# Merge with tokens on partitions, the three products of a weight chunk sorted, and the retention output's transposes placed later

## The chip, the cores and the metric

The kernel runs on one core of one Trainium2 chip. The metric is the device time of one execution in microseconds (us); smaller is better. Before the change three executions took 2119.16, 2122.03 and 2122.19 us, median 2122.03.

The engines are named as in the profile: PE is TensorE's matrix multiply and PEld its weight load, DVE is VectorE, ACT is ScalarE, SP issues the transfers. A matrix product on PE has a stationary operand (128 x 128, put into the array by a weight load) and a moving operand (128 x N, streamed through it); the result stands in PSUM with the stationary operand's columns on its partitions.

## What is computed

Two layers over 256 tokens of width 2048. In each layer one normalised input `h` feeds two branches, retention (8 heads) and latent attention (16 heads); each branch has its own projection back to 2048 columns, the two are gated by sigmoids, summed, and projected once more:

```
proj = h @ w_in
rq, rk, rv, rg, cq, ckv, kr, mg, bg = jnp.split(proj, points, axis=-1)
o_ret = head_group_norm(retention(rq, rk, rv)).reshape(B, S, RET_V_W)
y_ret = (o_ret * jax.nn.silu(rg)) @ w_ret_proj
...
y_mla = (o_mla * jax.nn.silu(mg)) @ w_mla_proj
g_a, g_b = jnp.split(jax.nn.sigmoid(bg), 2, axis=-1)
merged = g_a * y_ret + g_b * y_mla
out = merged @ w_out
return x + gate[:, None, :] * out
```

All is f32.

## The kernel before

**Products in three parts.** Every weight and every activation is split into a rounded part (`hi`, of type fp32r) and the rest (`lo`). `mm3` (L258) makes a product out of three: hi·hi (L260), hi·lo (L261) and lo·hi (L262), all added in the same place of PSUM.

**Weights come in chunks.** `load_split` (L246) fetches one chunk of 512 KB into a tile `wst` (a pool of 5, L237), ACT writes its hi half (L241) and DVE its lo half (L242) into a tile `whl` (a pool of 3). A chunk is two row blocks of 128 by 512 columns. SP issues all transfers of weights in program order.

**Two layouts.** `proj` (L274) takes a 128 x 128 block of weights as the stationary operand and streams the 256 tokens: results have features on partitions, and a chunk makes 24 products of 256 columns (2 row blocks x 4 column blocks x 3). `proj_tok` (L282) takes 128 tokens of the activation as the stationary operand and streams 512 columns of weights: results have tokens on partitions, and a chunk makes 12 products of 512 columns (2 row blocks x 2 token halves x 3). Before the change `proj_tok` makes the retention values and gates (`rv`, `rg`) and most of the last output; `proj` makes the rest: the gate columns `C_BA` (tiles `ma`, L480), the retention projection (`branch_a`, L639), the gate columns `C_BB` (L873) and the attention projection (L877). Each of these four takes 4 pieces of 512 columns, each of 8 chunks, in either layer.

**Order of the work.** The code is written in program order and a scheduler then orders each engine's instructions by a simulated time. In a layer come: the first products (`first_products`, L580; it makes 14 of 16 column groups, two of them `ma`), then the retention of four pairs of heads (`g` = 0 to 3, L703 to L752), with other products between (`run(PLAN[...])`: `a` is `gate_a`, `b` is `branch_a`, `q`, `r` and `v` belong to attention), then the attention heads, then the merge (L870 to L882), then `w_out`. After its head pair's norm and gate (`rv*rg`, L743), retention turns its result by eight transposes on PE (L749), whose outcome is split into the tiles `z` (L750). `PLAN[4]` is `"a3 b0 b1 b2 b3"`; `branch_a` needs the `z` of all four pairs, the last one for its chunks 7 and 8.

**Background.** In layer 0 `bg()` puts pieces of the modulation's product (`w_mod`, `mod_slice` L400: one load into `wst`, two DVE instructions at L341 into `macc`) between the chunks, 0.6 of one to each chunk while the `b` projections run and 0.5 in the merge.

Of the kernel before, what the change touches and what calls it, by code (L numbers as in the profile page):

```python
# [17 lines left out]
P = 128  # L18
# [90 lines left out]
def trunk(ctx: ExitStack, tc: tile.TileContext, x, c, positions, w_mod, b_mod, g_norm, w_in, g_cq,  # L109
# [153 lines left out]

    def proj_chunk(accs, hi, lo, k0, nk, span, act):

        for k in range(nk):
            kt = k0 + k
            for j in range(hi.shape[2] // P):
                cs = slice(j * P, (j + 1) * P)
                mm3(accs[j // 2][:, j % 2, :], (hi[:, k, cs], lo[:, k, cs]),  # L270
                    act.block(kt),
                    start=(kt == span[0] and j % 2 == 0), stop=(kt == span[1] - 1))
# [9 lines left out]
    def proj_tok(w, col, act, span=(0, KT)):  # L282

        accs = [acc_tile() for _ in range(2)]
        for k0 in range(*span, 2):
            hi, lo = load_split(w[k0 * P : (k0 + 2) * P, col : col + 512], 2, 512)
            for k in range(2):
                kt = k0 + k
                for t in range(2):
                    mm3(accs[t].rearrange("p a b -> p (a b)"), act.block(kt, slice(t * P, (t + 1) * P)),  # L290
                        (hi[:, k, :], lo[:, k, :]), start=kt == span[0], stop=kt == span[1] - 1)
        return [a.rearrange("p a b -> p (a b)") for a in accs]
# [175 lines left out]
    class Slots(dict):  # L468


        def __missing__(self, key):
            self[key] = (tokens if key[0] in ("rv", "rg") else blocks)(key[0])
            return self[key]

    def ret_proj(W, n, hh, span=(0, KT)):
# [3 lines left out]
        if n >= 12:  # L479
            return proj(W, C_BA + (n - 12) * 512, 512, hh, span)  # L480
        return proj_tok(W, C_RV + (n - 4) * 512, hh, span)

    def ret_dst(tiles, n):
# [4 lines left out]
        if n >= 12:  # L488
            return [tiles["ma", n - 12][:, 2 * a : 2 * a + 2, :] for a in range(2)]
        t = tiles[("rv", n - 4) if n < 8 else ("rg", n - 8)]  # L490
# [120 lines left out]
    def layer(l, r, u):  # L611
# [90 lines left out]

        for sg in range(2):  # L703
            for which in range(2):
                get(2 * sg + which, rope_pair)
            run(PLAN[2 * sg])
            for pr in range(2):
# [36 lines left out]
                for h in range(2):  # L744
                    ps = aux_tile()
                    for e in range(2):
                        for t in range(2):
                            f = h * S + e * P
                            T.transpose(ps[:, e * S + t * P : e * S + (t + 1) * P], rv[:, t, f : f + P], ident)  # L749
                    split_into(*zz.flat(2 * g + h), ps)  # L750
                if pr == 0:
                    run(PLAN[2 * sg + 1])  # L752

# [7 lines left out]
        for name in PLAN[4:]:  # L761
            run(name)
# [6 lines left out]
        for g in range(MH // 2):  # L769
# [12 lines left out]
            for k0 in (0, 2):  # L782
# [6 lines left out]
                split_into(hr, lr, w[:, :, :, NOPE:])  # L789
                for k in range(2):  # L790
                    kt = k0 + k
                    b = cq.block(kt)
                    for h in range(2):
                        mm3(a1[:, h, :], (hn[:, k, h, :], ln[:, k, h, :]), b, kt == 0 and h == 0, kt == 3)
                    mm3(a2[:, 0, :], tuple(u[:, k].rearrange("p h d -> p (h d)") for u in (hr, lr)), b, kt == 0, kt == 3)
# [5 lines left out]
            for k0 in (0, 2):  # L801
                hi, lo = load_split(w_ukv[l, k0 * P : (k0 + 2) * P, g * 512 : (g + 1) * 512], 2, 512)
                for k in range(2):
# [3 lines left out]
                    for h in range(2):  # L807
                        mm3(a1[:, h, :], (hv[:, h, :NOPE], lv[:, h, :NOPE]), b, kt == 0 and h == 0, kt == 3)
                    for t in range(2):
                        ts = slice(t * P, (t + 1) * P)  # L810
# [193 lines left out]
```

## Time and profile before

| | |
|---|---|
| median of three runs | 2122.03 us |
| the profiled execution's own time | 2121.04 us |
| its span in the profile | 2119.2 us |
| PE busy | 2067.8 us, 98% of the span |
| DVE, ACT busy | 1505.7 us (71%), 1062.0 us (50%) |
| transfers | 460.99 MB, mean 218 GB/s |

A product's row gives its own duration from first column to last result. Products overlap, so the pace is read from the start of one to the start of the next, or from the number of products in a stretch in which PE never rests.

### The profile page before, as it was taken

The numbers are of one execution on the slowest core, as the hardware profiler recorded it, in microseconds if no ns is written. First come the engines' busy times: TensorE is split into PE (matmuls) and PEld (weight loads), VectorE is DVE, ScalarE is ACT, GpSimd is POOL, SyncE is SP. The second block draws the span as 40 slices with busy tenths as digits, with TensorE's granted clock in tenths as the row PEclk, the third lists the DMA queues.
The fourth block names the chain that finished last, engine by engine and source line by source line (L and its number), as shares of the span: only waits on it lengthen the run. The fifth ranks groups of instructions, "written<-read, shape, count | busy, mean of one in ns | idle before, by whom it ended". The sixth has DMA issues, their size and how long they took to land.

```text
span 2119.2 us, 37911 instructions
## 1 busy us (share of the span) xinstructions
PE 2067.8 (98%) x15418; PEld 1964.6 (93%) x15422; DVE 1505.7 (71%) x2258; ACT 1062.0 (50%) x1485; POOL 0.2 (0%) x4
## 2 busy tenths in 40 slices
PE   7999999998999999999999999999999999999998
PEld 4898898998999999999998799899999999999987
DVE  5789987677677876775577776657766777754464
ACT  4554356543356664444454464445443666644453
POOL 0000000000000000000000000000000000000000
PEclk9999999999999999999999999999999999999999
DMA  8988866566766667776569976665567666666572
GB/s 309 313 297 284 296 188 186 160 200 209 265 207 195 184 204 239 254 257 194 184 182 326 311 218 186 189 180 157 185 221 225 186 193 195 204 216 186 181 240 97
DMA packets 263535, 460.99 MB, mean 218 GB/s; under 512 B 18464, under 2 KB 68032, under 8 KB 263360
## 3 DMA queue, kind: packets, MB, share of 16 engines
q1 hardware_dynamic: 263360, 458.57, 68.8%
q8 instruction: 121, 1.98, 0.4%
q14 instruction: 54, 0.44, 0.1%
HBM read 456.41 MB, written 2.10 MB: 216 GB/s over the span
## 4 chain that ended last, share of the span: by engine, by line
PE 72%; DMA 14%; DVE 9%; issue 3%; ACT 1%; SPq 0%; ACTq 0%; DVEq 0%
PE acc L261 22%; PE acc L262 22%; PE acc L260 22%; DMA wst<-in_w_mod 9%; DMA ring<-in_w_mod 4%; DVE whl L242 4%; DVE macc L341 2%; DMA wmod<-in_w_mod 1%; DVE tmp L341 1%; ACT whl L241 1%; PE aux L262 1%; PE aux L261 1%; PE aux L260 1%; DVE extra L341 0%; PE aux L857 0%
## 5 line engine op out<-in xcount | busy, mean ns | idle before, releaser
L241 ACT ACTIVATE whl<-wst 128x1024 fp32r<-128x1024 f32 (+1 forms) x708 | 707.9, 1006 | 821.2 <-PE acc L262 674.1
L242 DVE TENSOR_TENSOR whl<-wst,whl 128x1024 fp32r<-128x1024 f32 (+1 forms) x708 | 812.6, 1155 | 310.8 <-ACT whl L241 309.3
L260 PE MATMUL acc<-h,whl 128*128 128x256 f32 x2272 | 645.2, 285 | 3.8 <-DVE qkn L465 1.2
L261 PE MATMUL acc<-h,whl 128*128 128x256 f32 x2272 | 643.6, 284 | 0.8 <-DVE h L242 0.8
L262 PE MATMUL acc<-h,whl 128*128 128x256 f32 x2272 | 638.6, 284 | 2.4 <-DVE whl L242 2.2
L260 PEld LDWEIGHTS acc<-h,whl 128*128 128x128 f32 x2272 | 436.2, 192 | 6.0 <-ACT h L241 1.6
L261 PEld LDWEIGHTS acc<-h,whl 128*128 128x128 f32 x2272 | 436.5, 192 | 2.0 <-DVE h L242 1.4
L262 PEld LDWEIGHTS acc<-h,whl 128*128 128x128 f32 x2272 | 433.5, 192 | 3.9 <-DVE whl L242 3.8
L262 PE MATMUL acc<-z,whl 128*128 128x256 f32 x1024 | 291.5, 285 | 6.5 <-DVE whl L242 6.4
L261 PE MATMUL acc<-z,whl 128*128 128x256 f32 x1024 | 291.1, 285 | 2.6 <-DVE z L242 2.6
L260 PE MATMUL acc<-z,whl 128*128 128x256 f32 x1024 | 291.4, 285 | 1.7 <-ACT ma L622 1.7
L341 DVE SCALAR_TENSOR_TENSOR macc<-wst,cact,macc 128x512 f32<-128x512 f32 x180 | 134.9, 749 | 133.4 <-DMA wst<-in_w_mod 131.3
L261 PE MATMUL acc<-whl,h 128*128 128x512 f32 x512 | 203.6, 398 | 3.2 <-DVE whl L242 3.1
L262 PEld LDWEIGHTS acc<-z,whl 128*128 128x128 f32 x1024 | 197.1, 193 | 8.6 <-DVE whl L242 8.4
L261 PEld LDWEIGHTS acc<-z,whl 128*128 128x128 f32 x1024 | 197.5, 193 | 2.9 <-DVE z L242 2.8
L262 PE MATMUL acc<-whl,h 128*128 128x512 f32 x512 | 200.1, 391 | 0.0
L260 PEld LDWEIGHTS acc<-z,whl 128*128 128x128 f32 x1024 | 197.3, 193 | 2.1 <-ACT ma L622 2.0
L260 PE MATMUL acc<-whl,h 128*128 128x512 f32 x512 | 181.0, 391 | 0.0
L341 DVE SCALAR_TENSOR_TENSOR tmp<-ring,cact,tmp 128x512 f32<-128x512 f32 x150 | 112.2, 750 | 44.7 <-DMA ring<-in_w_mod 43.1
L261 PEld LDWEIGHTS acc<-whl,h 128*128 128x128 f32 x512 | 96.2, 188 | 26.5 <-DVE whl L242 7.2
L260 PEld LDWEIGHTS acc<-whl,h 128*128 128x128 f32 x512 | 96.0, 188 | 19.8
L262 PEld LDWEIGHTS acc<-whl,h 128*128 128x128 f32 x512 | 96.3, 188 | 19.2
(265 smaller groups left out, 2701.2 us busy)
## 6 DMA issues: line engine op xcount, KB each, us to landing
wst<-in_w_in SPq DMA_DIRECT2D x416, 512.0 KB, 4.4
wst<-in_w_mod SPq DMA_DIRECT2D x96, 512.0 KB, 4.2
ring<-in_w_mod SPq DMA_DIRECT2D x80, 512.0 KB, 5.2
wst<-in_w_ret_proj SPq DMA_DIRECT2D x64, 512.0 KB, 5.0
wst<-in_w_mla_proj SPq DMA_DIRECT2D x64, 512.0 KB, 4.9
wst<-in_w_out SPq DMA_DIRECT2D x64, 512.0 KB, 4.8
wst<-in_w_ukv SPq DMA_DIRECT2D x32, 512.0 KB, 3.9
wst<-in_w_uq SPq DMA_DIRECT2D x32, 384.0 KB, 4.2
```

What stands on the lines that cost most here:

```text
L241: A.activation(hi, src, AF.Copy)
L242: V.tensor_tensor(lo, src, hi.bitcast(F32), ALU.subtract)
L260: T.matmul(o, a[0], b[0], start=start, stop=False, skip_group_check=True)
L261: T.matmul(o, a[0], b[1], start=False, stop=False, skip_group_check=True)
L262: T.matmul(o, a[1], b[0], start=False, stop=stop, skip_group_check=True)
L341: V.scalar_tensor_tensor(acc, w[:, k, :], cact[:, k0 + k : k0 + k + 1], acc, ALU.mult, ALU.add)
```

## The change

It has four parts. (1) `ma`, the retention projection, the `C_BB` gates and the attention projection use `proj_tok`. (2) The merge then has its sum with tokens on partitions, and turns it by eight transposes for each piece of 512 columns before it is split into `m`; before, no transposes were needed. (3) `chunk` replaces `mm3` for weights: for a whole chunk first all products with the hi half of the weights (L270), then all with the lo half (L273). (4) Retention's transposes move into `turn`, called later in the program: for pairs 0 and 2 after `run(PLAN[2 * sg + 1])`, for pair 1 after the `q` product, for pair 3 after `a3`.

```diff
+    def chunk(todo):
+        for o, w, a, start, _, moves in todo:
+            for i in range(2):
+                x, y = (a[i], w[0]) if moves else (w[0], a[i])
+                T.matmul(o, x, y, start=start and i == 0, stop=False, skip_group_check=True)
+        for o, w, a, _, stop, moves in todo:
+            x, y = (a[0], w[1]) if moves else (w[1], a[0])
+            T.matmul(o, x, y, start=False, stop=stop, skip_group_check=True)
...
-        if n >= 12:
-            return proj(W, C_BA + (n - 12) * 512, 512, hh, span)
-        return proj_tok(W, C_RV + (n - 4) * 512, hh, span)
+        return proj_tok(W, C_RV + (n - 4) * 512 if n < 12 else C_BA + (n - 12) * 512, hh, span)
...
-            accs = proj(w_ret_proj[l], n * 512, 512, zz)
-            for a in range(2):
-                s2 = ma[:, 2 * a : 2 * a + 2, :]
-                V.tensor_tensor(s2, s2, accs[a], ALU.mult)
+            for t, acc in enumerate(proj_tok(w_ret_proj[l], n * 512, zz)):
+                V.tensor_tensor(ma[:, t, :], ma[:, t, :], acc, ALU.mult)
...
+        def turn(g):
+            for h in range(2):
+                ps = aux_tile()
+                for e in range(2):
+                    for t in range(2):
+                        f = h * S + e * P
+                        T.transpose(ps[:, e * S + t * P : e * S + (t + 1) * P], tiles["rv", g][:, t, f : f + P], ident)
+                split_into(*zz.flat(2 * g + h), ps)
...
             run(PLAN[2 * sg])
+            if sg:
+                turn(1)
...
                 V.tensor_tensor(rv, rv, rg, ALU.mult)
-                for h in range(2):
-                    ps = aux_tile()
...
                 if pr == 0:
                     run(PLAN[2 * sg + 1])
+                    turn(g)
...
-        for name in PLAN[4:]:
-            run(name)
+        last, *rest = PLAN[4].split()
+        run(last)
+        turn(3)
+        run(" ".join(rest))
...
-            accs = proj(W, C_BB + n * 512, 512, hh)
             gb = [tmp_tile(), tmp_tile()]
+            for t, acc in enumerate(proj_tok(W, C_BB + n * 512, hh)):
+                A.activation(gb[t], acc, AF.Sigmoid)
+            for t, acc in enumerate(proj_tok(w_mla_proj[l], n * 512, zz)):
+                V.tensor_tensor(gb[t], gb[t], acc, ALU.mult)
+                V.tensor_tensor(gb[t], gb[t], tiles["ma", n][:, t, :], ALU.add)
             for a in range(2):
-                A.activation(gb[a], accs[a].rearrange("p a b -> p (a b)"), AF.Sigmoid)
-            accs = proj(w_mla_proj[l], n * 512, 512, zz)
...
+                ps = aux_tile()
+                for b in range(2):
+                    f = (2 * a + b) * P
+                    for t in range(2):
+                        T.transpose(ps[:, b * S + t * P : b * S + (t + 1) * P], gb[t][:, f : f + P], ident)
+                split_into(*mm.flat(2 * n + a), ps)
```

The other users of `mm3` on weights (`proj_chunk`, `proj_tok`, the two products of an attention head pair, the last output's third piece) call `chunk` in the same way.

How the instructions stand is shown at three places. First PE in layer 0, around the transposes of the last head pair (g = 3). Before, the last products of `b0`'s sixth chunk stand ahead of them:

```order
L260 MATMUL acc<-z,whl 128x256
L261 MATMUL acc<-z,whl 128x256
L262 MATMUL acc<-z,whl 128x256
L749 MATMUL aux<-cst,rv 128x128 x8
L347 LDWEIGHTS part
```

After (L270 is hi, L273 is lo, L737 is the last score product of this pair, L709 the transposes):

```order
L737 MATMUL aux<-rv,tmp 128x256
L270 MATMUL acc<-whl,z 128x512 x4
L273 MATMUL acc<-whl,z 128x512 x4
L270 MATMUL acc<-whl,z 128x512 x8
L273 MATMUL acc<-whl,z 128x512 x4
L270 MATMUL acc<-whl,z 128x512 x8
L273 MATMUL acc<-whl,z 128x512 x4
L270 MATMUL acc<-whl,z 128x512 x8
L273 MATMUL acc<-whl,z 128x512 x4
L709 MATMUL aux<-cst,rv 128x128 x8
```

Before, 83 products of 256 columns stood between the last score product (L726) and the transposes; now 44 of 512 columns do, and as 84 `z` products now stand ahead of the transposes, where `b0` has 72 that need no `z` of the last pair, one chunk of `b1` has come ahead of them.

Second, DVE at the same place. Before, the gate product `rv*rg` (L743), for which the transposes wait, stands behind a background row (L341):

```order
L741 TENSOR_SCALAR rv<-rv,small 128x256 x4
L242 TENSOR_TENSOR whl<-wst,whl 128x1024
L341 SCALAR_TENSOR_TENSOR macc<-wst,cact,macc 128x512
L743 TENSOR_TENSOR rv<-rv,rg 128x1024
L242 TENSOR_TENSOR whl<-wst,whl 128x1024
```

After (L346 is the background row, L752 and L754 the norm and `rv*rg`):

```order
L346 SCALAR_TENSOR_TENSOR macc<-wst,cact,macc 128x512
L752 TENSOR_SCALAR rv<-rv,small 128x256 x4
L242 TENSOR_TENSOR whl<-wst,whl 128x1024
L754 TENSOR_TENSOR rv<-rv,rg 128x1024
L346 SCALAR_TENSOR_TENSOR macc<-wst,cact,macc 128x512 x2
L242 TENSOR_TENSOR whl<-wst,whl 128x1024
```

The background row now stands ahead of the norm, and two more stand between `rv*rg` and the next weight split.

Third, PE where the merge of layer 0 goes from its first piece to the second. Before, the products of the attention projection (`z`) were followed at once by those of the next gates (`h`), and no transposes stood there. After (L895 are the new transposes, L352 background sums):

```order
L273 MATMUL acc<-whl,z 128x512 x4
L270 MATMUL acc<-whl,h 128x512 x8
L273 MATMUL acc<-whl,h 128x512 x4
L270 MATMUL acc<-whl,h 128x512 x8
L273 MATMUL acc<-whl,h 128x512 x4
L270 MATMUL acc<-whl,h 128x512 x6
L895 MATMUL aux<-cst,tmp 128x128 x2
L270 MATMUL acc<-whl,h 128x512 x2
L352 LDWEIGHTS part
L352 MATMUL aux<-ones_h,part 128x1
L273 MATMUL acc<-whl,h 128x512 x4
```

Two transposes stand behind 30 products of the next gates' first three chunks, the other six a little later. In the whole program 6144 products of 256 columns are gone and 3072 of 512 columns and 64 transposes are new.

## Rows read from the trace of the kernel before

**Rows 1.** Page, part 1: busy us, share of the span, instructions.

```profile
PE 2067.8 (98%) x15418; PEld 1964.6 (93%) x15422; DVE 1505.7 (71%) x2258; ACT 1062.0 (50%) x1485; POOL 0.2 (0%) x4
```

**Rows 2.** Groups of PE products by shape: busy us, mean ns | idle before.

```profile
L260 PE MATMUL acc<-h,whl 128*128 128x256 f32 x2272 | 645.2, 285 | 3.8 <-DVE qkn L465 1.2 <-ACT h L241 0.9 <-ACT h L543 0.9
...
L261 PE MATMUL acc<-whl,h 128*128 128x512 f32 x512 | 203.6, 398 | 3.2 <-DVE whl L242 3.1
```

**Rows 3.** Stretches holding one width of product only, then one with late weights.

```profile
core 0: us, PE busy (x) PEld busy (x) DVE busy (x) ACT busy (x) POOL busy (x), PEclk, DMA share, GB/s
1890.00:2010.00 120.00, 120.00 (x1002) 120.00 (x1001) 58.08 (x54) 49.62 (x52) 0.00 (x0) 1.00 0.62 184
150.00:180.00 30.00, 30.00 (x134) 24.87 (x133) 28.04 (x36) 11.70 (x11) 0.00 (x0) 1.00 0.93 312
...
1180.00:1224.00 44.00, 42.08 (x183) 33.69 (x182) 33.29 (x41) 19.27 (x22) 0.00 (x0) 1.00 0.92 315
```

**Rows 4.** PE in order of time around eight transposes in layer 1.

```profile
1541.12 0.28 PE L262 MATMUL acc<-z,whl 128*128 128x256 f32 x1
1541.24 1.04 PE L749 MATMUL aux<-cst,rv 128*128 128x128 f32 x8
1542.03 0.36 PE L260 MATMUL acc<-z,whl 128*128 128x256 f32 x1
1542.23 0.29 PE L261 MATMUL acc<-z,whl 128*128 128x256 f32 x1
```

**Rows 5.** Waits: us in total, times, longest us.

```profile
ACT whl L241 <- PE acc L262: 674.1, 387, 5.5
...
DVE macc L341 <- DMA wst<-in_w_mod: 131.3, 70, 4.5
...
PEld acc L262 <- DVE whl L242: 12.2, 17, 2.1
...
PE acc L262 <- DVE whl L242: 8.7, 12, 1.9
...
PEld acc L261 <- DVE whl L242: 7.2, 11, 1.7
...
ACT whl L241 <- DMA wst<-in_w_mla_proj: 4.2, 2, 2.6
...
PE acc L261 <- DVE whl L242: 3.1, 4, 1.3
...
ACT whl L241 <- DMA wst<-in_w_ret_proj: 2.8, 1, 2.8
```

**Rows 6.** PE's groups in layer 0 from 498 to 516 us.

```profile
L260 PE MATMUL acc<-z,whl 128*128 128x256 f32 x21 | 7.0, 342 | 1.7 <-ACT ma L622 1.7
L261 PE MATMUL acc<-z,whl 128*128 128x256 f32 x21 | 6.7, 321 | 0.0
L262 PE MATMUL acc<-z,whl 128*128 128x256 f32 x21 | 6.6, 317 | 0.0
L749 PE MATMUL aux<-cst,rv 128*128 128x128 f32 x8 | 2.0, 428 | 4.5 <-DVE rv L743 4.5
L347 PE MATMUL aux<-ones_h,part 128*128 128x1 bf16 x12 | 0.5, 169 | 0.0
```

**Rows 7.** DVE in order of time at that place.

```profile
502.59 1.22 DVE L242 TENSOR_TENSOR whl<-wst,whl 128x1024 fp32r<-128x1024 f32 x1
504.85 0.75 DVE L341 SCALAR_TENSOR_TENSOR macc<-wst,cact,macc 128x512 f32<-128x512 f32 x1 [1.04 <-DMA wst<-in_w_mod]
505.52 1.22 DVE L743 TENSOR_TENSOR rv<-rv,rg 128x1024 f32<-128x1024 f32 x1
```

**Rows 8.** Stretches of layer 0: that place, two of the `b` projections, one of the merge.

```profile
498.00:516.00 18.00, 11.80 (x83) 11.24 (x82) 12.94 (x23) 6.47 (x8) 0.00 (x0) 0.72 0.68 215
516.00:550.00 34.00, 34.00 (x294) 33.96 (x294) 25.29 (x31) 13.88 (x14) 0.00 (x0) 1.00 0.71 231
550.00:590.00 40.00, 37.12 (x316) 36.67 (x315) 25.48 (x31) 14.57 (x17) 0.00 (x0) 1.00 0.79 259
860.00:900.00 40.00, 37.91 (x312) 37.35 (x311) 24.95 (x29) 14.79 (x16) 0.00 (x0) 1.00 0.80 264
1134.00:1168.00 34.00, 34.00 (x152) 28.16 (x151) 27.37 (x32) 16.33 (x20) 0.00 (x0) 1.00 0.96 331
```

**Rows 9.** Groups of DVE and ACT in the merge and in the splits.

```profile
L242 DVE TENSOR_TENSOR whl<-wst,whl 128x1024 fp32r<-128x1024 f32 x636 | 774.4, 1222 | 307.8 <-ACT whl L241 306.3
...
L879 DVE TENSOR_TENSOR tmp<-tmp,acc 128x512 f32<-128x512 f32 x16 | 10.7, 684 | 0.0
...
L880 DVE TENSOR_TENSOR tmp<-tmp,ma 128x512 f32<-128x512 f32 x16 | 10.6, 686 | 0.0
```

More of the change, by code (lines that the diff above doesn't have):

```diff
@@ L262, in mm3 @@
         T.matmul(o, a[1], b[0], start=False, stop=stop, skip_group_check=True)
-    def proj_chunk(accs, hi, lo, k0, nk, span, act):
[L266 to L272, printed above, removed]
+    def chunk(todo):
[6 more added lines that the diff above has]
+            T.matmul(o, x, y, start=False, stop=stop, skip_group_check=True)
+    def proj_chunk(accs, hi, lo, k0, nk, span, act):
+        chunk([(accs[j // 2][:, j % 2, :], (hi[:, k, j * P : (j + 1) * P], lo[:, k, j * P : (j + 1) * P]),
+                act.block(k0 + k), k0 + k == span[0] and j % 2 == 0, k0 + k == span[1] - 1, False)
+               for k in range(nk) for j in range(hi.shape[2] // P)])
     def proj(w, col, n, act, span=(0, KT)):
@@ L286, in proj_tok @@
             hi, lo = load_split(w[k0 * P : (k0 + 2) * P, col : col + 512], 2, 512)
[L287 to L291, printed above, removed]
+            chunk([(accs[t].rearrange("p a b -> p (a b)"), (hi[:, k, :], lo[:, k, :]),
+                    act.block(k0 + k, slice(t * P, (t + 1) * P)), k0 + k == span[0], k0 + k == span[1] - 1, True)
+                   for k in range(2) for t in range(2)])
         return [a.rearrange("p a b -> p (a b)") for a in accs]
@@ L487, in ret_dst @@
             return [tiles["qk", n // 2 * 2 + a][:, f : f + 2, :] for a in range(2)]
-        if n >= 12:
-            return [tiles["ma", n - 12][:, 2 * a : 2 * a + 2, :] for a in range(2)]
-        t = tiles[("rv", n - 4) if n < 8 else ("rg", n - 8)]
+        t = tiles[("rv", n - 4) if n < 8 else ("rg", n - 8) if n < 12 else ("ma", n - 12)]
         return [t[:, a, :] for a in range(2)]
@@ L793, in layer @@
                     for h in range(2):
-                        mm3(a1[:, h, :], (hn[:, k, h, :], ln[:, k, h, :]), b, kt == 0 and h == 0, kt == 3)
-                    mm3(a2[:, 0, :], tuple(u[:, k].rearrange("p h d -> p (h d)") for u in (hr, lr)), b, kt == 0, kt == 3)
+                        todo.append((a1[:, h, :], (hn[:, k, h, :], ln[:, k, h, :]), b, kt == 0 and h == 0, kt == 3, False))
+                    w = [u[:, k].rearrange("p h d -> p (h d)") for u in (hr, lr)]
+                    todo.append((a2[:, 0, :], w, b, kt == 0, kt == 3, False))
+                chunk(todo)
             A.activation(qn, a1[:, :, 0:P], AF.Copy)
@@ L807, in layer @@
                     for h in range(2):
[L808 removed]
+                        todo.append((a1[:, h, :], (hv[:, h, :NOPE], lv[:, h, :NOPE]), b, kt == 0 and h == 0, kt == 3, False))
                     for t in range(2):
[L810 to L812 removed]
+                        todo.append((a2[:, t, :], (hv[:, :, NOPE:], lv[:, :, NOPE:]),
+                                     [u[:, t * P : (t + 1) * P] for u in b], kt == 0 and t == 0, kt == 3, True))
+                chunk(todo)
             A.activation(kn, a1[:, :, 0:P], AF.Copy)
@@ L949, in last_output @@
             hi, lo = load_split(w[k0 * P : (k0 + 4) * P, c0 : c0 + 256], 4, 256)
-            for k in range(k0, k0 + 4):
-                for t in range(2):
-                    mm3(accs[t], mm.block(k, slice(t * P, (t + 1) * P)), (hi[:, k - k0], lo[:, k - k0]), k == 0, k == KT - 1)
+            chunk([(accs[t], (hi[:, k - k0], lo[:, k - k0]), mm.block(k, slice(t * P, (t + 1) * P)), k == 0, k == KT - 1, True)
+                   for k in range(k0, k0 + 4) for t in range(2)])
         for t in range(2):
```

16 lines of the change are left out of this document (3 added, 13 removed).

## The prediction

> **What bounds the kernel now.** I read the engines' busy shares first, then PE's groups, then stretches with a single kind of product, then the waits, then the one place where PE rests long.
>
> PE is busy for 98% of the span, DVE for 71%, ACT for 50% [rows 1]. A busy PE says little by itself, because a product's row (285 ns for 256 columns, 398 ns for 512) is longer than its share of the stream [rows 2]. So I take the pace from stretches that hold one kind only and in which PE never rests [rows 3]. In the first, 1002 products of 256 columns touch 120 us; the row also counts those that only reach over the edges, about two, so the pace is 120/1000 = 0.120 us. In the second, 134 products of 512 columns touch 30 us, which gives 30/132.3 = 0.2268 us. The two stretches have the same clock (1.00) and very different transfer rates (184 and 312 GB/s), so neither is waiting for weights. At 0.120 us a chunk of 24 narrow products takes 2.88 us, against 1.06 us of ACT and 1.22 us of DVE for its split [rows 9].
>
> The waits say the same: ACT waits 674.1 us in total for PE to give a weight tile back, so weights normally lie ready [rows 5]. The kernel is bound by PE's stream of products; other things matter only where they make it pause. The pauses are few: those for DVE's half of the weights (`whl`) add up to 11.8 us as PE's idle time (8.7 and 3.1) or 19.4 us as its weight loads see them (12.2 and 7.2), and one place in layer 0, at 498 to 516 us, stands out [rows 5, 6, 8].
>
> **Wide products for narrow ones.** 6144 products of 256 columns become 3072 of 512 with the same arithmetic. Two narrow ones take 0.2400 us, a wide one 0.2268 us: 0.0132 us saved 3072 times is **40.6 us**. The new products have just the form of those in the second stretch (activation stationary, `whl` streamed), so I take its pace. The ends are 0.226 us (about 43 us saved) and the pace of the third stretch of [rows 3], where wide products wait for weights: 44/181.3 = 0.243 us, at which nothing is saved. The stretches in question are nearer to the first end: in the `b` projections and the merge PE's idle time is 0 to 2.9 us in 34 to 40 us [rows 8].
>
> The Trainium skill, "TensorE: Matmul & The Clock Gate", section "Back-to-back issue gap", gives for a product alone columns/2.4 + 2.5 ns when the clock is full, which is 109.2 and 215.8 ns. By it a pair would save only 2.5 ns, 7.7 us in all. The trace differs: both widths run 11 ns above it, and it is this constant, paid once where it was paid twice, that makes most of the 40.6 us.
>
> **The merge's transposes.** Eight for each of four pieces in two layers: 64 on PE. Between the product that starts at 1541.12 and the one at 1542.23 lie 1.11 us; they hold eight transposes and two products' shares, so the eight take 1.11 - 0.24 = 0.87 us, 0.109 us each [rows 4]. That is **7.0 us** more of PE's stream. Below nothing is excluded, since it is added work on the full engine.
>
> The same page, section "Part 4: PE-mode transpose", tells of some 275 ns for one in a kernel. That speaks against the change and would make 17.6 us of the 7.0. Here 1.04 us for a row of eight contradicts it as a pace.
>
> The transposes also add a wait: PE stands still until DVE has summed, and behind them on PE stand the next piece's products, for which ACT and DVE wait in turn. In layer 0, 30 products (6.8 us) stand between the last product and the first two transposes, and 36 (8.2 us) before the other six. DVE's chain for all of it is two multiplications, a sum, a weight split, a background subtraction (taken as 0.69 us like the sum), a sum: 2 x 0.684 + 0.686 + 1.222 + 0.69 + 0.686 = 4.65 us, the first sum after 2.05 us [rows 9]. So 3.5 us of slack are left. The work on DVE and ACT does not change otherwise: the same number of multiplications, sums and splits of the same size.
>
> **The sorted chunk.** Before, DVE's half is needed at the second or third product, 0.23 or 0.24 us after the chunk begins. Now it is needed after 16 narrow (1.92 us) or 8 wide ones (1.81 us), some 1.6 us later. The waits for it are 2.1 us at the longest and mostly below 1 us (12.2 us in 17) [rows 5], so nearly all go. The bounds are 0, if ACT's half is late at the same places, and 19.4 us; I take **14 us**, between the two readings. Number and order of loads on SP stay nearly the same, so no transfer starts later by it.
>
> **Retention's transposes.** They wait for DVE only at one place: pair 3 of layer 0, 4.5 us [rows 6]. DVE's `rv*rg` stood there behind a background row that waited 1.04 us for its transfer [rows 7], and the granted clock fell: 0.72 on the mean of these 18 us [rows 8]. At full pace the work in it would take 63 x 0.120 + 0.87 + 0.5 = 8.9 us, so the place costs 9.1 us [rows 6]. The name of the change promises cover here, but the order of instructions gives little: 83 narrow products stood between the last score product and the transposes (10.0 us), now 44 wide ones do (10.0 us). What does change is DVE's order, in which the background row comes before the norm; against that, one chunk of `b1` now stands ahead of the transposes, whose split is queued behind two more background rows. The bounds are 0 and 9.1 us; I take **4 us** saved.
>
> Elsewhere the transposes already start behind finished work, and moving them gains nothing. For pair 3 of layer 1 the cover shrinks, from 115 narrow products (13.8 us) to 48 wide ones (10.9 us). With this and the eight new waits in the merge I put **3 us** of new pauses into the sum, bounds 0 and 12 (1.5 us each, the size of a mean wait for a background transfer, 131.3/70 = 1.9 us, less what slack takes).
>
> **The sum.** 2121.0 - 40.6 + 7.0 - 14 - 4 + 3 = 2072.4 us for the profiled execution. The median of the runs lies 1.0 above it, so 2073.
>
> **Rivals.**
>
> *Pauses only move (chance 0.20).* Sorting and later transposes gain nothing net; the counts of products remain: 2121.0 - 40.6 + 7.0 + 3 = 2090. For it: DVE's lateness comes from transfers (131.3 us of waiting [rows 5]), which the change leaves alone.
>
> *Weights set the pace (0.12): no gain.* A wide chunk takes 12 x 0.2268 = 2.72 us instead of 2.88, so the same transfers must come 6% faster. If `wst` tiles come free too late, chunks keep their old pace, the saving is nil and the transposes fall into the waits: about 2115 to 2121. For it: ACT does wait for some loads (2.8 and 4.2 us [rows 5]) and PE rests in two of the stretches. Against: 259 GB/s would become 275, and the trace has 331 GB/s with PE busy throughout [rows 8].
>
> *The merge's transposes stop PE (0.07): slower.* If DVE is over 3.5 us late at each of the eight, because background rows ahead of the sums wait for transfers (4.5 us at the longest [rows 5]), and each such stop brings the clock down as at 498 us, each costs 9.1 us: 2072.4 - 3 + 8 x 9.1 = 2142. The change is slower from 6.4 us each (51.6/8) on. Against: mean waits of 1.9 us stay below the slack.
>
> *The forecast (0.61)*, own range 2060 to 2086.
>
> **How the numbers follow.** The low end takes all bounds of a gain, 2121.0 - 43 + 7.0 - 19.4 - 9.1 = 2056. The high end leaves half the saving and no gain of pauses: 2121.0 - 20 + 7.0 = 2108. That leaves out most of the second and all of the third rival, and so under 2 in 10. A measurement of this kernel tells about 0.2% (4 us) from no change. Faster: the forecast, the first rival and most of the second, 0.90; same: the rest of the second, 0.04; slower: 0.06.
>
> **What the profile of the changed kernel would show.** The wide groups' pace in undisturbed stretches of the `b` projections near 0.227 us, else the first term is wrong. PE's waits for DVE's `whl` down from 11.8 us to 1 or 2, else sorting missed its mark. At pair 3 of layer 0, a wait for `rv*rg` below 4.5 us and a granted clock that stays at 1.00; a mean as low as 0.72 there would say that nothing was gained. The new transposes' idle time below 3 us in all. ACT waiting for `wst` transfers for tens of us would speak for the second rival. The prediction would be wrong above all if the wide products of the merge ran at 0.24 us or more.

## The result and the profile after

The changed kernel takes 2106.54 us (median of four, 2103.23 to 2107.54) against 2122.11 us (2119.16 to 2122.94) before: a ratio of 0.992, interval 0.9901 to 0.994, or 15.6 us. Forecast were 49. The profiled execution has a span of 2105.8 us, 13.4 less than before; the readings below are made on it.

Page of the kernel after, part 1, to be set against [rows 1]:

```profile
PE 2045.3 (97%) x12410; PEld 1806.7 (86%) x12414; DVE 1505.9 (72%) x2258; ACT 1060.1 (50%) x1489; POOL 0.2 (0%) x4
```

3008 PE instructions are gone (15418 to 12410): 3072 products fewer, 64 transposes more. DVE and ACT do what they did. PE rests 60.5 us of the span (2105.8 - 2045.3), 9.1 more than before (2119.2 - 2067.8 = 51.4).

Waits of the kernel after, as in [rows 5] (L346 is the background row, L270 a product with the hi half, L273 with the lo half):

```profile
DVE macc L346 <- DMA wst<-in_w_mod: 138.8, 74, 6.3
...
PEld acc L273 <- DVE whl L242: 37.2, 44, 2.3
...
PE acc L273 <- DVE whl L242: 21.1, 25, 1.8
...
ACT whl L241 <- DMA wst<-in_w_ret_proj: 15.8, 8, 3.3
...
ACT whl L241 <- DMA wst<-in_w_in: 14.7, 6, 3.9
...
ACT whl L241 <- DMA wst<-in_w_mla_proj: 13.8, 8, 2.7
...
PE acc L270 <- ACT whl L241: 4.3, 3, 3.5
```

Two things turned the wrong way. PE waits 21.1 us for DVE's half of the weights, against 11.8 before. ACT waits 44.3 us for transfers of weights (15.8, 14.7 and 13.8), against 13.2 (2.8 and 4.2 [rows 5], and 6.2 in this row of before):

```profile
ACT whl L241 <- DMA wst<-in_w_in: 6.2, 3, 2.5
```

To see where, I cut both spans at the same marks: the first `z` product of the `b` projections, the first product of the attention, the first `z` product of the merge, the first `m` product, in either layer. Before (columns as in [rows 3]); the stretches are the work up to the first `z`, the `b` projections of layer 0, the merge of layer 0, the merge of layer 1:

```profile
0.00:480.40 480.40, 461.21 (x3006) 412.25 (x3007) 382.82 (x561) 242.54 (x307) 0.20 (x4) 0.99 0.77 249
480.40:591.90 111.50, 101.76 (x831) 99.95 (x830) 79.46 (x116) 42.69 (x50) 0.00 (x0) 0.95 0.73 237
...
822.70:991.80 169.10, 165.43 (x1382) 163.02 (x1381) 110.73 (x128) 69.91 (x76) 0.00 (x0) 1.00 0.75 242
...
1856.00:2017.90 161.90, 161.83 (x1348) 161.59 (x1348) 83.70 (x82) 68.00 (x72) 0.00 (x0) 1.00 0.64 194
```

The same four stretches after:

```profile
0.00:481.60 481.60, 460.87 (x2623) 393.44 (x2624) 382.24 (x560) 240.31 (x305) 0.20 (x4) 0.98 0.77 248
481.60:588.10 106.50, 97.87 (x446) 78.50 (x445) 79.72 (x117) 44.24 (x53) 0.00 (x0) 0.95 0.73 243
...
820.20:991.90 171.70, 161.84 (x734) 128.15 (x733) 110.76 (x128) 69.17 (x76) 0.00 (x0) 1.00 0.73 239
...
1847.90:2003.70 155.80, 155.75 (x699) 128.86 (x700) 83.69 (x81) 67.40 (x72) 0.00 (x0) 1.00 0.63 202
```

The first stretch lost 383 rows, each worth 0.0132 us, and so should be 5.1 us shorter; it is 1.2 longer. The second should be 5.1 shorter (385 rows) and is 5.0. The merge of layer 1, where PE rests 0.05 us, is 6.1 shorter. The merge of layer 0, with the same products, is 2.6 us longer: PE rests 9.9 us there (171.70 - 161.84) against 3.7 before. The five remaining stretches together are 6.1 us shorter. So of some 33.6 us by the counts, about 8.7 are lost in the merge of layer 0 (6.1 as in layer 1, and 2.6), about 6.3 before the first `z`, and the rest, some 5, in small parts elsewhere. The 14 us that sorting should add do not show in this sum; the runs below take the change apart.

### The profile page after: what moved, and what is told of

Its sections match the earlier page's. It is cut to its first block, busy times and chain, and to the rows that moved or that the text cites. A ratio compares the mean times of both kernels' runs of the same rounds, so it can differ in the third digit from the quotient of the medians.

```text
span 2105.8 us, 31895 instructions
## 1 busy us (share of the span) xinstructions
PE 2045.3 (97%) x12410; PEld 1806.7 (86%) x12414; DVE 1505.9 (72%) x2258; ACT 1060.1 (50%) x1489; POOL 0.2 (0%) x4
## 5 line engine op out<-in xcount | busy, mean ns | idle before, releaser
L270 PE MATMUL acc<-whl,h 128*128 128x512 f32 x2048 | 513.6, 391 | 0.9 <-DVE rv L606 0.7
L270 PEld LDWEIGHTS acc<-whl,h 128*128 128x128 f32 x2048 | 381.6, 188 | 79.8 <-issue 1.7
L270 PE MATMUL acc<-h,whl 128*128 128x256 f32 x2432 | 331.0, 287 | 8.6 <-ACT h L241 3.8
L270 PEld LDWEIGHTS acc<-h,whl 128*128 128x128 f32 x2432 | 310.0, 194 | 12.5 <-ACT h L241 5.0
L273 PE MATMUL acc<-whl,h 128*128 128x512 f32 x1024 | 281.8, 395 | 8.5 <-DVE whl L242 8.1
L270 PE MATMUL acc<-whl,z 128*128 128x512 f32 x1024 | 256.7, 392 | 3.8 <-ACT whl L241 3.8
L346 DVE SCALAR_TENSOR_TENSOR macc<-wst,cact,macc 128x512 f32<-128x512 f32 x180 | 135.0, 750 | 140.9 <-DMA wst<-in_w_mod 138.8
L273 PEld LDWEIGHTS acc<-whl,h 128*128 128x128 f32 x1024 | 188.8, 188 | 53.9 <-DVE whl L242 16.9
L270 PEld LDWEIGHTS acc<-whl,z 128*128 128x128 f32 x1024 | 192.8, 189 | 44.7 <-ACT whl L241 4.5
L273 PE MATMUL acc<-h,whl 128*128 128x256 f32 x1216 | 175.1, 284 | 0.0
L273 PEld LDWEIGHTS acc<-h,whl 128*128 128x128 f32 x1216 | 159.1, 193 | 0.1
L273 PE MATMUL acc<-whl,z 128*128 128x512 f32 x512 | 139.8, 395 | 13.2 <-DVE whl L242 13.1
L346 DVE SCALAR_TENSOR_TENSOR tmp<-ring,cact,tmp 128x512 f32<-128x512 f32 x150 | 112.0, 751 | 51.4 <-DMA ring<-in_w_mod 49.9
L273 PEld LDWEIGHTS acc<-whl,z 128*128 128x128 f32 x512 | 95.2, 189 | 39.2 <-DVE whl L242 20.3
L270 PE MATMUL acc<-c,whl 128*128 128x256 f32 x640 | 102.7, 289 | 1.0 <-DVE ma L643 1.0
L270 PEld LDWEIGHTS acc<-c,whl 128*128 128x128 f32 x640 | 86.8, 191 | 1.3 <-ACT q L241 1.2
L270 PE MATMUL acc<-m,whl 128*128 128x256 f32 x512 | 67.3, 283 | 0.0
L270 PEld LDWEIGHTS acc<-m,whl 128*128 128x128 f32 x512 | 64.0, 192 | 0.1
L270 PE MATMUL acc<-whl,m 128*128 128x512 f32 (+1 forms) x256 | 56.5, 365 | 0.0
L273 PE MATMUL acc<-c,whl 128*128 128x256 f32 x320 | 56.0, 283 | 0.0
```

The lines of the kernel that those rows point to most:

```text
L270: T.matmul(o, x, y, start=start and i == 0, stop=False, skip_group_check=True)
L273: T.matmul(o, x, y, start=False, stop=stop, skip_group_check=True)
L346: V.scalar_tensor_tensor(acc, w[:, k, :], cact[:, k0 + k : k0 + k + 1], acc, ALU.mult, ALU.add)
```

## The experiments

A negative change is a gain; times are medians. Runs of different batches are compared by their ratio to the kernel before, run on the same chip in the same batch; 0.001 is 2.1 us.

**The parts of the change, each alone.** `unsorted` is the changed kernel with the old order within a chunk.

```diff
     def chunk(todo):
-        for o, w, a, start, _, moves in todo:
-            for i in range(2):
...
+        for o, w, a, start, stop, moves in todo:
+            x, y = (a, w) if moves else (w, a)
+            mm3(o, x, y, start, stop)
```

> The change without its sorting: the three products of a place stand together again, the rest (tokens on partitions, later transposes) stays. Theory 1 (loads and DVE set the pace of PE wherever background loads run between the weights, so a faster product only waits longer): sorting is a buffer of some 1.6 us for DVE's half and does little where loads are late; 2104 to 2114 us, PE's waits for DVE's weight half about as long as in the changed kernel or a little longer. Theory 2 (sorting itself costs: the scheduler, seeing that the lo half is needed later, puts its split later on DVE): 2090 to 2098 us and fewer waits.

Measured: 2104.26 us, 0.992 [0.9902, 0.9937]. That is the ratio of the whole change: in it, sorting is worth nothing in total, to within some 5 us by the two intervals. In single stretches it is not nothing. The merge of layer 0 in `unsorted`:

```profile
819.60:984.00 164.40, 160.44 (x733) 128.36 (x732) 111.27 (x128) 69.22 (x76) 0.00 (x0) 1.00 0.76 250
```

With the same products and five tiles this merge takes 164.4 us, 4.7 less than before, where the sorted kernel takes 171.7, 7.3 more. The same pair with retention's transposes at their old place (`tokens_only` and `turn_back`, below) takes 163.5 and 171.0. ACT's waits for the chunks' transfers add up to 13.1 us in `unsorted`, against 44.3 after. As the whole spans are only 2.2 us apart (2103.6 and 2105.8), sorting gains about 5 us in other stretches. Such figures come from one trace each: `turn_only`, whose merge PE and ACT run in the same order as before, takes 165.5 us there in place of 169.1.

`sort_only` is the kernel before with that function `chunk` for its weights, and nothing else.

> The kernel before with nothing but the sorted chunk. Theory 1: 2112 to 2122 us, as the waits of 11.8 us for DVE's half go away in part. Theory 2: 2128 to 2138 us, more waits for DVE's half than before. My prediction's term for this part alone was -14 us, 2108.

Measured: 2120.61 us, 0.9994 [0.9985, 1.0004]. Waits of `sort_only`:

```profile
ACT whl L241 <- DMA wst<-in_w_ret_proj: 19.0, 8, 3.1
...
PE acc L273 <- DVE whl L242: 7.9, 10, 2.8
...
PE aux L754 <- DVE rv L748: 5.1, 1, 5.1
```

PE's waits for DVE's half fall from 11.8 to 7.9 us, not to 1 or 2, and the wait at pair 3 grows from 4.5 to 5.1 us. Ten waits are left, up to 2.8 us long: DVE's half is then later than the 1.6 us that the order covers. And ACT's waits for the chunks' transfers rise from 13.2 to 28.4 us (19.0, 5.5 and 3.9): measured by ACT's need they come later than before, though the layout, and with it PE's work per chunk, is the old one.

`tokens_only` is the kernel before with the new layout and the merge's transposes alone; `turn_back` is the changed kernel with retention's transposes at their old place (below); `turn_only` is the kernel before with the new place alone.

```diff
                 V.tensor_tensor(rv, rv, rg, ALU.mult)
+                turn(g)
...
-            if sg:
-                turn(1)
...
-                    turn(g)
...
-        turn(3)
```

> The kernel before with nothing but tokens on partitions in the four products and the merge's transposes. The counts of products say -33.6 us, 2088 us; where the loads and DVE's order take a part of it, 2100 to 2106 us, as the version that also has the later transposes (2104 us).

> The changed kernel with retention's transposes at their old place in the program, everything else changed. If the later place gave nothing, as the counts of products ahead of the transposes say: within 3 us of the changed kernel (2104 to 2110 us). If the chunk of the second retention projection that now stands ahead of the last pair's transposes costs a pause of its own (3.7 and 2.0 us in the trace, and a lower clock), the pause at 505 us changes its form and it is 3 to 8 us faster. If the later place did gain, it is 5 to 10 us slower.

> The kernel before with the later place of retention's transposes alone: old layout, old order within a chunk. Theory (the later place is worth something because the token layout leaves too little cover at the old one; in the old layout 83 and 115 narrow products stood there anyway): between 2113 and 2121 us, at most the 9.1 us that pair 3 of layer 0 costs before. Rival (the later place brings the same 9 to 13 us whatever the layout): 2107 to 2111 us. In the profile, pair 3 of layer 0 would show with 131 narrow products in place of 83 ahead of the transposes and a wait for rv below 1 us under either; what tells them apart is whether anything beyond those 9.1 us goes.

Measured: `tokens_only` 2117.76 us, 0.9978 [0.9965, 0.9991]; `turn_back` 2115.96 us, 0.9981 [0.9966, 0.9996]; `turn_only` 2115.38 us, 0.9982 [0.997, 0.9994]. PE at pair 3 of layer 0 in `tokens_only`:

```profile
503.53 0.59 PE L731 MATMUL aux<-rv,tmp 128*128 128x256 f32 x2
503.77 0.58 PE L262 MATMUL acc<-whl,z 128*128 128x512 f32 x1
515.26 1.94 PE L705 MATMUL aux<-cst,rv 128*128 128x128 f32 x8 [10.91 <-DVE rv L748]
```

Only one product stands between the last score product (L731) and the transposes, and PE rests 10.9 us on the norm, the gate and the background rows ahead of them. In `turn_back` the same row waits 12.2 us. Before, the wait was 4.5 us behind 83 narrow products. So the layout and the later place belong together: 0.0022 and 0.0018 alone, 0.0080 together (`unsorted`). `tokens_only` missed both of its ranges; `turn_back` is 0.0061 slower than the changed kernel, some 13 us, more than the 5 to 10 of its third case. The new place alone gains 3.8 us (1.3 to 6.4), and its theory holds against the rival's 9 to 13.

**Is it the background?** `few_mod_after` and `few_mod_before` are the two kernels with 7 of 8 background pieces left out, so that the modulation lacks their part of its sum; `few_mod_unsorted` is the same without sorting.

```diff
-        if k0 + 2 == KT:
-            mod_finish(l, m0, 4, macc)
+        mod_finish(l, m0, 4, macc)
...
-            for k0 in range(0, KT, 2):
+            for k0 in range(0, KT, KT):
                 background.append(lambda l=l, m=m, k0=k0: mod_slice(l, m, k0))
```

> The changed kernel with seven of eight background pieces of the modulation left out (64 pieces in layer 0 and 32 in layer 1 become 8 and 4, so the result of the modulation is incomplete). Theory 1: the waits for weights in layer 0's projections and merge vanish, and it lies 34 to 42 us below the kernel before with the same left out (40.6 of wide products less 7.0 of transposes, and a few waits). Theory 2 or 3 (the later transposes cost): the distance stays near the 16 us of the full kernels.

> The kernel before with the same seven of eight background pieces left out (the result of the modulation is incomplete). Both theories: a few tens of us below 2122, since its waits for DVE's half and its pause at 506 us go. Theory 1: 2085 to 2105 us, and 34 to 42 us above the changed kernel with the same left out.

> The changed kernel without sorting and with 7 of 8 background pieces left out, so that the modulation's sum lacks them. To be compared with the same kernel sorted (2082.1 us, 0.9815 of before) and both with background (sorted 2106.5, unsorted 2104.3). Theory (sorting can hide lateness of up to 1.6 us only; without background loads DVE's half is hardly ever late, so there is nothing to hide): within 3 us of the sorted one, 0.980 to 0.983 of before. Rival A (sorting is worth its forecast in itself, the background spoils it): 0.986 to 0.990 of before. Rival B (sorting costs in itself): 0.979 of before or less.

Measured: `few_mod_after` 2082.05 us, 0.9815 [0.9799, 0.9831]; `few_mod_before` 2109.37 us, 0.9948 [0.993, 0.9966]; `few_mod_unsorted` 2089.01 us, 0.9848 [0.9835, 0.9862]. Without background the change gains 0.0133, some 28 us, against 0.008 with it: more, but short of the 34 to 42 that theory 1 expected. The merge of layer 0 in `few_mod_before`, then in `few_mod_after`:

```profile
825.50:986.80 161.30, 161.30 (x1346) 161.30 (x1345) 79.43 (x75) 66.94 (x70) 0.00 (x0) 1.00 0.61 183
```

```profile
819.80:974.90 155.10, 155.10 (x698) 128.50 (x697) 79.76 (x75) 66.34 (x70) 0.00 (x0) 1.00 0.61 190
```

PE never rests in either, and the change takes 6.2 us. With background the same merge has 7.8 us more before (169.1), 9.4 more in `unsorted` (164.4 against 155.0) and 16.6 more after (171.7): here part of the expected gain went, and nearly all of that with the sorted chunk.

On sorting, neither side was right as written. With no background loads it gains 0.0033, 7 us, half its forecast and between the theory's range and rival A's; in the profiled executions, whose spans differ by 3.7 us (2084.9 and 2081.2), the `b` projections of layer 0 take 109.4 us unsorted and 105.5 sorted, while the merge of layer 0 takes 155.0 and 155.1.

**What delays the merge.** DVE of the kernel after, in order of time:

```profile
857.82 0.75 DVE L346 SCALAR_TENSOR_TENSOR macc<-wst,cact,macc 128x512 f32<-128x512 f32 x1
...
862.55 0.75 DVE L346 SCALAR_TENSOR_TENSOR macc<-wst,cact,macc 128x512 f32<-128x512 f32 x1 [1.65 <-DMA wst<-in_w_mod]
863.22 1.22 DVE L242 TENSOR_TENSOR whl<-wst,whl 128x1024 fp32r<-128x1024 f32 x1
```

SP's queue there:

```profile
858.60 0.37 SPq L237 DMA_DIRECT2D wst<-in_w_mod  x1
```

And PE:

```profile
860.80 2.00 PE L270 MATMUL acc<-whl,h 128*128 128x512 f32 x8
864.50 1.20 PE L273 MATMUL acc<-whl,h 128*128 128x512 f32 x4 [1.70 <-DVE whl L242]
```

SP issues the background load only at 858.60, 0.03 us after DVE has ended its previous background row (857.82 + 0.75 = 858.57); I read that as the tile coming free. It lands about 3.9 us later; DVE's next background row waits for it, the split of a weight chunk stands behind that row, and PE, which has already done the eight hi products, waits 1.70 us for the split. This suggested two cures: a sixth tile, so that the load starts earlier, or the background rows later in DVE's queue.

`wst6` is the changed kernel with six `wst` tiles (and 30 large tiles in place of 31, for the room); `before_wst6` the kernel before with the same two lines.

```diff
-BIG = 31
-WP = 5
+BIG = 30
+WP = 6
```

> The changed kernel with six tiles for arriving weights instead of five (one of the 31 general tiles given up for it). Theory A (the loads of the background come late because SP can issue one only when a tile of the five is free again, and DVE, which frees it, waits for an earlier one): the stalls in layer 0's merge (171.7 us from its first product of z to the first of m) fall to about 160 us, and the whole to 2088 to 2096 us. Theory B (DVE's order: a background row stands ahead of the split and waits for a transfer that takes its 4 us whatever the number of tiles): within 3 us of the changed kernel, 2103 to 2110 us. The missing general tile could by itself cost a few us.

> The kernel before with six wst tiles in place of five (and 30 big tiles in place of 31). In the changed kernel the same edit took 13.4 us. Theory (the changed kernel asks for its chunks 6% faster, and only so do five tiles come free too late in the merge of layer 0; the 7.8 us of pauses there before are the same thing, smaller): 4 to 8 us gained, 2112 to 2117 us, almost all in the merge of layer 0 (169.1 us before). Rival (the sixth tile is worth the same 13 us to either kernel, so late tiles say nothing about why the change fell short): 2107 to 2109 us. Third (no gain at all before): 2119 to 2122 us.

Measured: `wst6` 2093.11 us, 0.9863 [0.9845, 0.9881]; `before_wst6` 2115.35 us, 0.9981 [0.9963, 0.9999]. The merge of layer 0 in `wst6`:

```profile
818.10:979.00 160.90, 158.93 (x733) 128.24 (x732) 109.10 (x126) 69.01 (x76) 0.00 (x0) 1.00 0.76 255
```

It takes 160.9 us in place of 171.7, with PE's rest down from 9.9 to 2.0 us. To the kernel before the sixth tile is worth some 4 us, to the changed one some 12 (0.992 to 0.9863). ACT's waits for the chunks' transfers fall from 44.3 to 1.2 us. So the sorted kernel got its transfers too late with five tiles. Faster chunks alone do not bring that about: `unsorted` has them and five tiles, and its merge takes 164.4 us. Whether the kernel before was short of tiles too, as its theory says, is not shown: its merge falls from 169.1 to 164.6 us with six, but takes 165.5 in `turn_only` with five. And with six tiles the scheduler also puts DVE's instructions of this merge in another order; no run tells the two apart.

`late_rows` is the changed kernel with five tiles and the DVE rows of a background piece one piece later in the program than its load.

```diff
-        mod_rows(macc, w, k0, 2)
-        if k0 + 2 == KT:
-            mod_finish(l, m0, 4, macc)
+        held.append((l, m0, k0, w))
+        if len(held) > 1:
+            mod_late()
```

> The changed kernel in which DVE's rows of a background piece come one background piece later in the program than its load, so that the load has landed when DVE comes to it; the number of tiles stays five, and the load holds its tile longer. Theory B: layer 0's merge falls to about 158 us and the whole to 2090 to 2098 us. Theory A: no better or worse, 2105 to 2120 us, since one of the five tiles is held longer.

Measured: 2098.3 us, 0.9891 [0.987, 0.9911], the merge of layer 0 166.0 us. It helps too, by less than theory B has (its bounds are 2098 us and a merge of 158) and against theory A. A held piece keeps its tile longer: ACT's waits for the chunks' transfers stay at 43.5 us (23.3, 11.4 and 8.8).

**Sorting with tiles in time.**

> The changed kernel with six wst tiles and with the old order within a chunk (hi, lo, hi for each block in place of all hi first). With five tiles the sorted order cost 2.3 us. Theory (sorting only hides what is late by up to 1.6 us, and with six tiles little is late, so that it makes no difference by itself): within 3 us of the run with six tiles, 2090 to 2096 us. Rival A (sorting is worth its 14 us once loads are in time): 2100 to 2107 us. Rival B (sorting costs, since all lo products at the end make a chunk hold its tile longer): below 2090 us.

> The kernel before with the sorted chunk and six wst tiles, in the old layout. Six tiles alone gave 0.9981 of before, sorting alone 0.9994. PE's waits for DVE's half stood at 11.8 us before and at 13.2 with six tiles. Theory (what sorting spares in waits comes back elsewhere because the scheduler places DVE's other work into the slack): within 3 us of six tiles alone, 0.997 to 0.9995. Rival (with loads in time sorting takes nearly all of these 13 us): 0.991 to 0.994 of before.

Measured: `wst6_unsorted` 2099.46 us, 0.9896 [0.987, 0.9921]; `sort_wst6` 2118.31 us, 0.9983 [0.9972, 0.9995]. In the token layout with six tiles sorting gains 0.0033, the size that it has without background, though here the two intervals overlap; the time lies between the theory's range and rival A's. In the old layout it gains nothing (0.9981 to 0.9983). Waits of `before_wst6`, then of `sort_wst6`:

```profile
PE acc L262 <- DVE whl L242: 8.5, 10, 1.9
...
PE acc L261 <- DVE whl L242: 4.7, 9, 1.2
...
PE aux L749 <- DVE rv L743: 2.3, 1, 2.3
```

```profile
PE aux L754 <- DVE rv L748: 7.5, 1, 7.5
...
PE acc L273 <- DVE whl L242: 6.2, 9, 1.9
```

The waits for DVE's half do fall, from 13.2 to 6.2 us; the wait at pair 3 grows from 2.3 to 7.5 us and takes 5.2 of these 7 back. That the scheduler's new order of DVE's rows causes it is likely, but was not tested by itself.

**Pair 3 of layer 0.** Two runs give it more cover, with PLAN's `a2` moved from behind pair 0 to the last group; the second has the later background rows besides.

```diff
-PLAN = ("a0 a1", "a2", "q", "r v", "a3 b0 b1 b2 b3")
+PLAN = ("a0 a1", "", "q", "r v", "a2 a3 b0 b1 b2 b3")
```

> The changed kernel with six wst tiles and PLAN's a2 moved from behind pair 0 to the last group, so that in layer 0 a chunk's worth of gate products without z (20 wide) and 72 z products stand ahead of pair 3's transposes in place of 44, in layer 1 75 in place of 48. With six tiles alone PE rested 6.3 us at pair 3 of layer 0 and its clock fell behind that. Theory (that place is short of cover, and its pause and clock are what is left to gain there): 6 to 11 us below the run with six tiles, 2082 to 2087 us, granted clock 1.00 at pair 3 of layer 0. Rival (the rest only moves, to pair 0, which loses a2 as its cover, or to the next wait): 2090 to 2097 us.

> The changed kernel with six wst tiles, a2 moved behind a pair 3 short of cover (as in the run wst6_a2late, 0.9875 of before), and DVE's rows of a background piece placed one piece later in the program than its load. Theory (tile shortage and rows queued ahead of the split are two faces of one delay, the background's transfer; with six tiles the later rows add little): 0.985 to 0.988 of before. Rival (the rows in DVE's queue are a cause of their own): their 8 us come on top, 0.982 to 0.984 of before, and PE's waits for DVE's half fall from 9.9 us to below 4.

Measured: `wst6_a2late` 2092.72 us, 0.9875 [0.9852, 0.9898]; `wst6_late_a2` 2094.17 us, 0.988 [0.9864, 0.9896]. Neither is better than `wst6`. The place itself in `wst6_a2late`:

```profile
498.00:516.00 18.00, 15.77 (x83) 11.67 (x82) 16.69 (x23) 9.80 (x12) 0.00 (x0) 1.00 0.73 249
```

The clock stays at 1.00, as its theory said, and the `b` projections of layer 0 fall from 107.0 us in `wst6` to 97.0. The merge of layer 0 gains another 3.7. But the work ahead of the `b` projections takes 2.4 us more and that between them and the merge 5.7, so that the profiled span is only 5.4 us shorter (2088.4 against 2093.8), and the medians of the runs, whose intervals overlap, show no gain: the rival's range holds the time. The place was right, the total wrong. In `wst6_late_a2` the `b` projections take 96.7 us, and PE still waits 10.3 us for DVE's half, against 9.9: the later rows add nothing to six tiles, so the two cures treat one delay, as the theory had it.

The best version found is `wst6`: 0.9863 of the kernel before, 29 us, where the change has 17 by the same measure (0.992).

## Why the prediction was wrong

**Wide products and the merge's transposes (-40.6 and +7.0): right.** PE in layer 1's merge, after:

```profile
1882.17 1.98 PE L270 MATMUL acc<-whl,h 128*128 128x512 f32 x8
...
1895.77 1.98 PE L270 MATMUL acc<-whl,z 128*128 128x512 f32 x8
```

Five chunks of twelve products take 13.60 us, 0.2267 us each; forecast was 0.2268. In the merge of layer 1, 1344 narrow products become 672 wide, 8.9 us less, and 32 transposes add 3.5: 5.4 us by the terms, 6.1 measured. By the formula for a product alone in the Trainium skill, "TensorE: Matmul & The Clock Gate", section "Back-to-back issue gap", an estimate for 672 pairs is 1.7 us saved, less than the transposes cost; the trace contradicts it for these streams.

The new transposes cost no pause. What the kernel after shows of their line:

```profile
L895 PE MATMUL aux<-cst,tmp x64: 270/272/332, 848.9 to 2012.0; 128*128 128x128 f32 x64
...
its engine sat idle before it (us, times) until:
  issue: 0.7, 2
  DVE tmp L889: 0.2, 1
```

The slack held, and the rival in which they stop PE falls. The 275 ns of the Trainium skill, "TensorE: Matmul & The Clock Gate", section "Part 4: PE-mode transpose", is near what a row lasts here (272 ns at the median), not what it adds to PE's stream (109 ns [rows 4]).

**The sorted chunk (-14): this step failed.** It said of the waits for DVE's half that "nearly all go", and that "Number and order of loads on SP stay nearly the same, so no transfer starts later by it". `sort_only` gained 1.3 us, sorting in the changed kernel nothing. The step took the lateness of before as given, and that failed in two ways. The new layout raised PE's waits for DVE's half from 11.8 us to 20.2 (`tokens_only`), and sorting left them there: 22.5 in `unsorted`, 21.1 after. And with sorting the transfers did come later: with five tiles ACT's waits for them rise from 13.2 to 28.4 us in the old layout, from 13.1 to 44.3 in the new, where the merge of layer 0 takes 7.3 us more for it. Where the transfers come in time, by six tiles or by leaving the background out, sorting gives 7 us in the new layout, half its term, and nothing in the old one with six tiles. How a new order on PE makes transfers late stays open: the scheduler also puts DVE's instructions of the merge in another order when the chunk is sorted, and no run tests that by itself.

**New pauses (+3, bounds 0 to 12): mis-sized.** Against the counts the merge of layer 0 lost 8.7 us and the work before the first `z` 6.3, already past the upper bound. The step looked for new pauses only at transposes. The merge of layer 0 looks like the rival "weights set the pace" confined to one stage: the chunks there kept their old pace (242 GB/s before, 239 after), and ACT waited for transfers for tens of us. But the rival's reason, that a wide chunk needs its transfers 6% faster, is not enough: `unsorted` runs the same wide chunks at 250 GB/s with five tiles. What cost the 7.3 us there was sorting, with five tiles and background loads. My reason against the rival, that the trace has 331 GB/s with PE busy [rows 8], holds for the rate and misses the point: in `wst6` the same merge runs at 255 GB/s and 10.8 us faster, so the rate was not short; the transfers came late. Without sorting the larger loss against the counts stands before the first `z` of layer 0: 485.9 us in `unsorted`, where the counts say 475.3.

**Retention's transposes (-4): gained nothing at the place named, and the step missed what they do.** PE at pair 3 of layer 0 after, then the same 18 us as in [rows 8]:

```profile
505.34 3.78 PE L270 MATMUL acc<-whl,z 128*128 128x512 f32 x8 [3.54 <-ACT whl L241]
510.73 2.08 PE L273 MATMUL acc<-whl,z 128*128 128x512 f32 x4 [1.61 <-DVE whl L242]
512.61 1.91 PE L709 MATMUL aux<-cst,rv 128*128 128x128 f32 x8
```

```profile
498.00:516.00 18.00, 12.85 (x55) 9.80 (x54) 14.07 (x29) 5.36 (x7) 0.00 (x0) 0.72 0.70 236
```

The transposes wait for nothing; the chunk of `b1` ahead of them does, 5.2 us in two pieces, and the clock's mean is 0.72 as before ([rows 8]). The prediction said what such a mean would say: that nothing was gained. Its danger, the chunk's split behind background rows, was named and then priced too low. ACT shows the first of the two:

```profile
503.19 0.21 ACT L302 ACTIVATE small<-small 128x4 f32<-128x4 f32 x1 [4.07 <-DVE small L745]
503.31 1.98 ACT L241 ACTIVATE whl<-wst 128x1024 fp32r<-128x1024 f32 x2
```

ACT's hi split stands behind the norm's square root (L302), which waits 4.07 us for DVE. "Moving them gains nothing" elsewhere was wrong in another way: I compared the cover before and after, not that of the new layout with the transposes left in place. There it falls to one product and costs 10.9 us in layer 0; the later place is what lets the layout's gain through.

**The work before the first `z` (no term): partly open.** PE's clock in four stretches, before and then after:

```profile
125.00:130.00 5.00, 4.54 (x37) 4.54 (x38) 4.71 (x7) 2.30 (x3) 0.00 (x0) 1.00 0.97 312
...
288.00:293.00 5.00, 5.00 (x44) 5.00 (x43) 1.73 (x3) 1.06 (x1) 0.00 (x0) 1.00 0.46 111
```

```profile
125.00:130.00 5.00, 4.92 (x28) 4.92 (x29) 2.79 (x5) 0.85 (x3) 0.00 (x0) 0.66 0.91 297
...
288.00:293.00 5.00, 4.13 (x18) 3.73 (x19) 3.66 (x6) 1.84 (x3) 0.00 (x0) 0.66 0.62 169
```

At two boundaries between groups of the first products the granted clock fell after the change and did not before: 0.34 of 5 us twice, by estimate 3.4 us. With 1.5 us more of rest (481.60 - 460.87 against 480.40 - 461.21) that makes 4.9 of the 6.3. It stays when the background is left out (446.9 us from the first product to the first `z` in `few_mod_after`, 443.9 in `few_mod_before`), so tiles and background pieces are not its cause. Nor is the clock its only cause: in `unsorted` it stands at 1.00 in both stretches, PE rests 23.2 us up to the first `z` in place of 19.2 before, and the stretch is longer still (485.9 us). That the modulation's own transfers set these boundaries is only a reading; no run tested it.

**The rivals.** "Pauses only move" came nearest in its mechanism and 16 us short in size. The result lies between it and "weights set the pace": one of four merges and `b` stretches kept its old time, the others gained.

## What to carry to other kernels

When the order or the length of the work on the bound engine changes, the transfers do not stay in time as they were: count the tiles between issue and release, not only the bytes per second. Take every part of a change out by itself and compare stretch by stretch: sorting was worth nothing in total, and in that total stood 7 us lost in one merge. A change that trades many products for few also removes cover from every wait that stands behind a number of products; compare the new layout with the old place, not only both ends. And a pause that is cured at one place is a gain only if the waits behind it do not grow: cutting the span at the same marks in both traces shows that in a few lines.

## What the runs showed of the hardware

In these two places the clock did not follow the length of PE's rests. PE of the kernel after at the first group boundary:

```profile
123.65 0.50 PE L270 MATMUL acc<-h,whl 128*128 128x256 f32 x2 [1.48 <-ACT h L241]
124.60 1.78 PE L270 MATMUL acc<-h,whl 128*128 128x256 f32 x7 [0.44 <-ACT whl L241]
```

Rests of 1.48 and 0.44 us stand ahead of a stretch with a mean granted clock of 0.66, that is partly at the lower of the two levels (1.2 GHz) and partly at the upper one (2.4 GHz). In `wst6_a2late` PE rests 2.23 us in the 18 us at pair 3, the longest rest being this:

```profile
505.25 1.20 PE L270 MATMUL acc<-whl,z 128*128 128x512 f32 x4 [1.66 <-ACT ma L623]
```

There the clock is 1.00, the upper level, throughout. A pause can so cost more than itself, or not, and only the clock's own column tells which.
